# Seven block products for the half-wide last chunk of three gated networks

## The chip, the cores and the metric

The kernel runs on one NeuronCore of a Trainium2 chip. The metric is the device time of one execution in microseconds (us). Before the change it is 1073.06 us, the median of 3 runs (1071.64 to 1073.41). Names of engines: PE is the matrix engine (PEld its weight loads), DVE the vector engine, ACT the scalar engine, POOL the general one, SP the queue that issues most DMAs.

## The reference, cut to what matters

The model has two layers. Each layer has two gated networks ("nets"), one at its start and one at its end, with a mixer and a cross attention between them. So there are four nets in all. The change touches the last three. All is in float32, with 256 tokens, width 1024 and an inner width of 2816:

```python
D_MODEL, SEQ, DEPTH, D_FF = 1024, 256, 2, 2816

def swiglu(x, w_gate, w_up, w_down):
    return (jax.nn.silu(x @ w_gate) * (x @ w_up)) @ w_down

for l in range(DEPTH):
    h = layer_norm(ALPHA * h + 0.5 * swiglu(h, ffn1_gate[l], ffn1_up[l], ffn1_down[l]), ...)
    ...                                   # mixer, cross attention
    h = layer_norm(ALPHA * h + 0.5 * swiglu(h, ffn2_gate[l], ffn2_up[l], ffn2_down[l]), ...)
```

## The kernel before, in words

**Products in three parts.** A float32 number is split into a high part (rounded to the matrix engine's fp32r format) and a low part (the rest). `split` (lines 61 and 62) does that: ACT casts the high part (`whi`), then DVE subtracts it from the source (`wlo`). A product is then high x high + high x low + low x high. Every weight tile of 128x1024 that comes from memory (`raw`, 512 KB, 6 buffers) costs one cast on ACT and one subtraction on DVE before PE can use it; there are 8 buffers each of `whi` and `wlo`. A raw buffer is free for the next load once DVE has read it for the last time.

**A net in chunks.** The inner width of 2816 is cut into chunks of 512 columns: five whole ones (numbers 0 to 4) and a last one (number 5) of 256. For each chunk PE computes x @ gate and x @ up, the result is activated and multiplied, and `turn` (line 446) turns it so that it can be the left operand of the down product: four DMAs deal it to other partitions (line 450), DVE transposes it (line 453), and it is split again (`ah`, `al`). The down product of a chunk goes in slabs of 256 inner columns (two raw tiles, 24 matmuls), `both(c, u)`. The order at the end of a net is written in the loop over chunks: chunk 4, slabs (2,1) and (3,0), chunk 5, slab (3,1), and then the tail with the three slabs (4,0), (4,1) and (5,0). In the tail each of the four output blocks (two halves of the tokens by two halves of the columns) takes its 6 matmuls of the first slab, 6 of the second and 6 of the third before the next block begins. After the first two blocks the first half of the tokens is normalised, and after the other two the second half (`finish`, line 303 on).

**Ways to do a chunk.** A whole chunk goes either directly (`hidden`, 96 matmuls of 512 columns) or by seven block products (`by_seven`, line 555). The latter is Strassen's scheme in Winograd's form on 2x2 blocks: x and the pair of gate and up are cut into halves of tokens, of model width, and into gate and up. Instead of eight products of blocks there are seven, of weights that are sums of blocks, against blocks of x that were summed beforehand (`blocks_of_x`). Each product is 12 matmuls (`run`, line 597). `parts_of` makes the weights of one product: it adds a second block where the product needs a sum (line 584, DVE, in place in the raw tile) and splits the result. `put` (line 606) makes the half sums of the seven results on DVE; the first copy is ACT's (line 612). What comes after the last product (the last three sums, the activation, the multiplication and `turn`) is in `left`, which the loop calls after the slab (c - 2, 1). Nets 2 to 4 do chunks 2 and 4 by seven (`sevens`, line 666), net 1 chunk 4 alone.

**The last chunk before the change** is `last_hidden` (line 641): it takes the weights as the left operand (`mm_cols`), so its result is turned already and needs neither DMAs nor transposes. Each of its four `mm_cols` is 8 matmuls of 512 columns and 8 of 256. It splits four raw tiles.

**The order of the work.** Each engine works off its instructions in an order that a planner fixes when the kernel is built: by the program's order as the priority, with an instruction held back until the planner expects its inputs. Where `manual_schedule` stands in the code, the program's order holds.

## Time and profile before

| what | value |
|---|---|
| median of 3 runs | 1073.06 us |
| the profiled execution | 1072.23 us |
| its span, first to last instruction | 1070.2 us |
| granted clock of PE | 0.998 |
| DVE, ACT, POOL busy | 946.3, 642.2, 65.0 us |
| mean DMA rate | 217 GB/s |

The profile gives times from the span's start. A line such as "L62" is line 62 of the kernel. A row of the timeline has the start, the time from the start to the end of the merged group, engine, line, operation, output<-inputs, shapes and count, and in brackets how long the engine had been idle and what it waited for. Rows of stretches ("A:B") have the length, then the busy time of each engine with its number of instructions, the granted clock, the DMA engines' busy share and GB/s. Chunk 5 of the four nets starts on PE at 146.41, 505.08, 672.71 and 1031.37 us.

### The profile page before, as it was taken

The numbers are of one execution on the slowest core, as the hardware profiler recorded it, in microseconds if no ns is written. First come the engines' busy times: TensorE is split into PE (matmuls) and PEld (weight loads), VectorE is DVE, ScalarE is ACT, GpSimd is POOL, SyncE is SP. The second block draws the span as 40 slices with busy tenths as digits, with TensorE's granted clock in tenths as the row PEclk, the third lists the DMA queues.
The fourth block names the chain that finished last, engine by engine and source line by source line (L and its number), as shares of the span: only waits on it lengthen the run. The fifth ranks groups of instructions, "written<-read, shape, count | busy, mean of one in ns | idle before, by whom it ended". The sixth has DMA issues, their size and how long they took to land.

```text
span 1070.2 us, 16314 instructions
## 1 busy us (share of the span) xinstructions
PE 1060.6 (99%) x5968; PEld 938.9 (88%) x5968; DVE 946.3 (88%) x1318; ACT 642.2 (60%) x916; POOL 65.0 (6%) x114
## 2 busy tenths in 40 slices
PE   9999999999999999999999999999999999999997
PEld 7888888889899888888888888888898998888886
DVE  6977997998998799999799999788989787999986
ACT  7556655767457565656575557566764665656660
POOL 9600001000000000000000000010000000000000
PEclk9999999999999999999999999999999999999999
DMA  9998395755575575948675875957536665759471
GB/s 360 259 298 269 119 281 167 251 188 159 177 271 168 181 247 198 292 167 226 236 260 192 250 261 173 298 168 227 190 128 208 247 230 176 259 151 341 133 220 40
DMA packets 130896, 231.90 MB, mean 217 GB/s; under 512 B 9409, under 2 KB 48609, under 8 KB 130817
## 3 DMA queue, kind: packets, MB, share of 16 engines
q1 hardware_dynamic: 129024, 228.49, 65.6%
q0 software_dynamic: 1216, 1.20, 0.5%
q8 instruction: 47, 0.77, 0.3%
q10 hardware_dynamic: 576, 1.18, 0.3%
q14 instruction: 33, 0.26, 0.1%
HBM read 216.15 MB, written 1.05 MB: 203 GB/s over the span
## 4 chain that ended last, share of the span: by engine, by line
PE 99%; DMA 0%; DVE 0%; issue 0%; DVEq 0%
PE acc L105 65%; PE dn L105 31%; PE acc L172 1%; PE dn L910 1%; DMA h<-in_x_dram 0%; PE dn L969 0%; PE dn L968 0%; PE dn L958 0%; PE acc L1034 0%; PE dn L472 0%; PE dn L875 0%; DVE h L358 0%; DVE h L353 0%; DVE st L338 0%; DVE h L326 0%
## 5 line engine op out<-in xcount | busy, mean ns | idle before, releaser
L61 ACT CAST whi<-raw 128x1024 fp32r<-128x1024 f32 (+1 forms) x438 | 442.4, 1042 | 199.3 <-DVE raw L584 54.7
L62 DVE TENSOR_TENSOR wlo<-raw,whi 128x1024 fp32r<-128x1024 f32 (+1 forms) x438 | 515.6, 1210 | 33.9 <-ACT whi L61 30.4
L105 PE MATMUL acc<-whi,xT 128*128 128x512 f32 x1032 | 312.9, 380 | 0.0
L105 PEld LDWEIGHTS acc<-whi,xT 128*128 128x128 f32 x1032 | 195.0, 189 | 27.5
L105 PE MATMUL acc<-wlo,xT 128*128 128x512 f32 x516 | 195.6, 379 | 0.0
L105 PE MATMUL acc<-xT,whi 128*128 128x512 f32 x576 | 142.2, 382 | 0.2
L105 PE MATMUL dn<-whi,ah 128*128 128x512 f32 x346 | 131.5, 380 | 0.0
L105 PE MATMUL dn<-wlo,ah 128*128 128x512 f32 x346 | 131.1, 379 | 0.0
L105 PE MATMUL dn<-whi,al 128*128 128x512 f32 x346 | 131.1, 379 | 0.0
L105 PEld LDWEIGHTS acc<-xT,whi 128*128 128x128 f32 x576 | 103.9, 190 | 12.5 <-ACT whi L61 0.7
L105 PEld LDWEIGHTS acc<-wlo,xT 128*128 128x128 f32 x516 | 97.5, 189 | 13.9
L105 PE MATMUL dn<-whi,xT 128*128 128x512 f32 x288 | 87.9, 381 | 0.0
L105 PEld LDWEIGHTS acc<-xT,wlo 128*128 128x128 f32 x576 | 75.5, 191 | 3.9
L105 PE MATMUL acc<-xT,wlo 128*128 128x256 f32 x576 | 75.9, 275 | 0.0
L105 PEld LDWEIGHTS dn<-wlo,ah 128*128 128x128 f32 x346 | 65.4, 189 | 9.2
L105 PEld LDWEIGHTS dn<-whi,al 128*128 128x128 f32 x346 | 65.4, 189 | 9.2
L105 PEld LDWEIGHTS dn<-whi,ah 128*128 128x128 f32 x346 | 65.4, 189 | 9.1
L584 DVE TENSOR_TENSOR raw<-raw 128x1024 f32<-128x1024 f32 x56 | 66.2, 1218 | 0.4
L350 POOL TENSOR_TENSOR rs<-rs,nhalf 128x1 f32<-128x1 f32 x16 | 14.9, 929 | 834.2 <-DVE rs L346 598.7
L105 PEld LDWEIGHTS dn<-whi,xT 128*128 128x128 f32 x288 | 54.6, 190 | 7.4
L105 PE MATMUL dn<-wlo,xT 128*128 128x512 f32 x144 | 54.6, 379 | 0.0
L332 DVE SCALAR_TENSOR_TENSOR h<-h,dn 128x512 f32<-128x512 f32 x31 | 21.2, 683 | 31.6 <-PE dn L105 31.6
(232 smaller groups left out, 1278.7 us busy)
## 6 DMA issues: line engine op xcount, KB each, us to landing
raw<-in_ffn_up_dram SPq DMA_DIRECT2D x88, 512.0 KB, 5.3
raw<-in_ffn_down_dram SPq DMA_DIRECT2D x88, 512.0 KB, 6.9
raw<-in_ffn_gate_dram SPq DMA_DIRECT2D x84, 512.0 KB, 5.0
raw<-in_w_in_dram SPq DMA_DIRECT2D x48, 512.0 KB, 4.7
dealt<-sg SPq DMA_DIRECT2D x80, 128.0 KB, 4.7
raw<-in_ca_k_dram SPq DMA_DIRECT2D x16, 512.0 KB, 5.1
raw<-in_w_out_dram SPq DMA_DIRECT2D x16, 512.0 KB, 4.3
raw<-in_ca_v_dram SPq DMA_DIRECT2D x16, 512.0 KB, 5.3
```

Of the source, the lines that this page charges most:

```text
L61: nc.scalar.copy(hi, src)
L62: lows.append(nc.vector.tensor_tensor(lo, src, hi.bitcast(F32), op=ALU.subtract))
L105: nc.tensor.matmul(o, w, x, start=start, stop=stop)
L172: nc.tensor.transpose(pt[:, k, :], src[:, (4 * j + k) * P : (4 * j + k + 1) * P], unit)
L332: nc.vector.scalar_tensor_tensor(v, v, ALPHA / scale, sums(y[i][n]), op0=ALU.mult, op1=ALU.add, accum_out=None if junk is None else st[:, ...
L350: nc.gpsimd.tensor_tensor(rs, rs, nhalf[:, 0:1], op=ALU.pow)
L584: nc.vector.tensor_tensor(r[i], r[i], plus[i], op=ALU.add)
L910: nc.tensor.matmul(o[g, hh, :], kc[:, hh, g], x, start=True, stop=True)
```

## The change

In nets 2 to 4 chunk 5 goes by seven as well. `by_seven` learns a width of 256: a block of weights (4 x 128 rows by 256 columns) then fits into a single raw tile, so each of the four blocks takes one of the six raw buffers, and the tiles that the whole chunks borrow (`spare0` to `spare2`, `lng`, `lnb`) aren't needed for weights. The half sums `e` and `f` go to `spare0` and `spare1` there, which are tiles of raw weights in the whole chunks. `turn` learns half the width. `last_hidden` remains for net 1.

```diff
-            def turn(s):
+            def turn(s, n=4):
                 ah, al = act_tiles()
-                x = fp.tile([P, 4, NT, P], F32, tag="dealt", name="dealt", bufs=1)
+                x = fp.tile([P, 4, NT, 32 * n], F32, tag="dealt", name="dealt", bufs=1)
                 for a in range(4):
-                    nc.sync.dma_start(x[a * 32 : a * 32 + 32], s[:, :, a * P : (a + 1) * P])
+                    nc.sync.dma_start(x[a * 32 : a * 32 + 32], s[:, :, a * 32 * n : (a + 1) * 32 * n])
...
             def by_seven(c0, bx):
+                ncol = min(CHUNK, DFF - c0)
+                whole = ncol == CHUNK
+                def block(m, j, *tags):
+                    to = []
+                    per = 2 if whole else 4
+                    for i, g in enumerate(tags if whole else tags[0:1]):
+                        r = (fp if "spare" in g else wp).tile([P, DM], F32, tag=g, name="raw", bufs=6 if g == "raw" else 1)
+                        r = r.rearrange("p (k c) -> p k c", c=ncol)
+                        a = (4 * j + per * i) * P
                         loads.append(nc.sync.dma_start(
-                            to[i], m[k * P : (k + 2) * P, c0 : c0 + CHUNK].rearrange("(k p) c -> p k c", p=P)
+                            r, m[a : a + per * P, c0 : c0 + ncol].rearrange("(k p) c -> p k c", p=P)
                         ))
...
-                w00 = block(gate, 0, pieces("spare0", "spare1"))
-                w01 = block(up, 0, pieces("lng", "lnb"))
-                w11 = block(up, 1, pieces("raw", "raw"))
-                w10 = block(gate, 1, pieces("spare2", "raw"))
+                w00 = block(gate, 0, *(("spare0", "spare1") if whole else ("raw",)))
+                w01 = block(up, 0, *(("lng", "lnb") if whole else ("raw",)))
+                w11 = block(up, 1, "raw", "raw")
+                w10 = block(gate, 1, *(("spare2", "raw") if whole else ("raw",)))
...
+                sums_of = [
+                    fp.tile([P, 4, P], F32, tag="up", name="half").rearrange("p k t -> p (k t)") if whole
+                    else fp.tile([P, DM], F32, tag=f"spare{n}", name="half", bufs=1)[:, 0:ncol] for n in range(2)
+                ]
...
-            sevens = (2, 4) if early is None else (4,)
+            sevens = (2, 4, 5) if early is None else (4,)
...
-                if c == max(sevens) + 1:
+                if c == len(chunks) - 1:
                     gb = ln_params(l, n)
```

The rest of the diff writes `ncol` for the fixed width of 512 in `run`, `parts_of` and `left`.

More of the change, by code (lines that the diff above doesn't have):

```diff
@@ L440, in gated @@
                     nc.vector.tensor_tensor(v, o, v, op=ALU.mult)
-            def turn(s):
+            def turn(s, n=4):
                 ah, al = act_tiles()
-                x = fp.tile([P, 4, NT, P], F32, tag="dealt", name="dealt", bufs=1)
+                x = fp.tile([P, 4, NT, 32 * n], F32, tag="dealt", name="dealt", bufs=1)
                 for a in range(4):
-                    nc.sync.dma_start(x[a * 32 : a * 32 + 32], s[:, :, a * P : (a + 1) * P])
+                    nc.sync.dma_start(x[a * 32 : a * 32 + 32], s[:, :, a * 32 * n : (a + 1) * 32 * n])
                 for i in range(NT):
-                    d = fp.tile([P, 4, P], F32, tag="up", name="square")
+                    d = fp.tile([P, 4, P], F32, tag="up", name="square")[:, 0:n, :]
                     nc.vector.transpose(
-                        d.rearrange("p k (b r) -> p b k r", b=4), x[:, :, i, :].rearrange("p b (k j) -> p b k j", k=4)
+                        d.rearrange("p k (b r) -> p b k r", b=4), x[:, :, i, :].rearrange("p b (k j) -> p b k j", k=n)
                     )
-                    split(ah[:, :, tok(i)], al[:, :, tok(i)], d)
+                    split(ah[:, 0:n, tok(i)], al[:, 0:n, tok(i)], d)
                 return ah, al
@@ L555, in by_seven @@
             def by_seven(c0, bx):
-                def rows_by_columns(r):
-                    return r.rearrange("p (k c) -> p k c", c=CHUNK)
-                def pieces(*tags):
-                    return [
-                        rows_by_columns(
-                            (fp if "spare" in g else wp).tile([P, DM], F32, tag=g, name="raw", bufs=6 if g == "raw" else 1)
-                        )
-                        for g in tags
-                    ]
-                def block(m, j, to):
-                    for i in range(2):
-                        k = 4 * j + 2 * i
+                ncol = min(CHUNK, DFF - c0)
[7 more added lines that the diff above has]
+                        a = (4 * j + per * i) * P
                         loads.append(nc.sync.dma_start(
-                            to[i], m[k * P : (k + 2) * P, c0 : c0 + CHUNK].rearrange("(k p) c -> p k c", p=P)
+                            r, m[a : a + per * P, c0 : c0 + ncol].rearrange("(k p) c -> p k c", p=P)
                         ))
+                        to.append(r)
                     return to
-                w00 = block(gate, 0, pieces("spare0", "spare1"))
-                w01 = block(up, 0, pieces("lng", "lnb"))
-                w11 = block(up, 1, pieces("raw", "raw"))
-                w10 = block(gate, 1, pieces("spare2", "raw"))
+                w00 = block(gate, 0, *(("spare0", "spare1") if whole else ("raw",)))
+                w01 = block(up, 0, *(("lng", "lnb") if whole else ("raw",)))
+                w11 = block(up, 1, "raw", "raw")
+                w10 = block(gate, 1, *(("spare2", "raw") if whole else ("raw",)))
                 def parts_of(r, plus=None):
                     hi, lo = [], []
-                    for i in range(2):
+                    for i in range(len(r)):
                         if plus is not None:
@@ L586, in parts_of @@
                         w = wp.tile([P, 1024], F32R, tag="wlo", name="wlo", bufs=8)
-                        h, w = (rows_by_columns(x) for x in (h, w))
+                        h, w = (x.rearrange("p (k c) -> p k c", c=ncol) for x in (h, w))
                         split(h, w, r[i])
@@ L590, in parts_of @@
                         lo.append(w)
-                    return Weights(hi, lo, 2, [])
+                    return Weights(hi, lo, 4 // len(r), [])
                 def part_of_x(i, j):
@@ L598, in run @@
                     for k in range(4):
-                        wh, wl = w.at(k, slice(0, CHUNK))
+                        wh, wl = w.at(k, slice(0, ncol))
                         mm_rows(o, x[0][:, k, :], x[1][:, k, :], wh, wl, k == 0, k == 3)
+                sums_of = [
+                    fp.tile([P, 4, P], F32, tag="up", name="half").rearrange("p k t -> p (k t)") if whole
+                    else fp.tile([P, DM], F32, tag=f"spare{n}", name="half", bufs=1)[:, 0:ncol] for n in range(2)
+                ]
                 def half_sum():
-                    return fp.tile([P, 4, P], F32, tag="up", name="half").rearrange("p k t -> p (k t)")
+                    return sums_of.pop(0)
                 def put(o, a, op, b):
@@ L608, in by_seven @@
                 s = activations()
-                g = [s[:, i, :] for i in range(NT)]
-                o = [acc((P, CHUNK)) for _ in range(4)]
+                g = [s[:, i, 0:ncol] for i in range(NT)]
+                o = [acc((P, ncol)) for _ in range(4)]
                 run(o[0], part_of_x(0, 0), parts_of(w00))
@@ L621, in by_seven @@
                 put(e, o[2], ALU.subtract, e)
-                o = [acc((P, CHUNK)) for _ in range(3)]
+                o = [acc((P, ncol)) for _ in range(3)]
                 run(o[0], bx[3], parts_of(w11))
@@ L631, in left @@
                         put(g[i], o[1 + i], ALU.add, g[i])
-                    s = fp.tile([P, NT, CHUNK], F32, tag="spare2", name="sg", bufs=1)
+                    s = fp.tile([P, NT, CHUNK], F32, tag="spare2", name="sg", bufs=1)[:, :, 0:ncol]
                     for i, u in enumerate((e, f)):
@@ L636, in left @@
                         nc.vector.tensor_tensor(v, v, u.rearrange("p (k a j) -> p k a j", a=4, j=32), op=ALU.mult)
-                    return turn(s)
+                    return turn(s, ncol // P)
                 return left
```

## The prediction

> **What bounds the kernel now.** I read the page's first part and its chain first, then the table of stretches around chunk 5, then the timelines of PE, DVE, ACT and SP there.

> ```profile
> PE 1060.6 (99%) x5968; PEld 938.9 (88%) x5968; DVE 946.3 (88%) x1318; ACT 642.2 (60%) x916; POOL 65.0 (6%) x114
> PE 99%; DMA 0%; DVE 0%; issue 0%; DVEq 0%
> ```

> PE is busy for 99% of the span and is the whole chain: what takes a matmul away shortens the kernel, as long as nothing else becomes late. DVE at 88% is the one that can. The mean says little, so here is the end of a net by stages (net 4; chunk 4 by seven, slabs (2,1) and (3,0), chunk 5), and chunk 5 of nets 2 and 3:

> ```profile
> 1002.88:1021.01 18.13, 18.13 (x85) 15.88 (x84) 18.13 (x21) 14.85 (x17) 0.00 (x0) 1.00 0.55 175
> 1021.01:1031.37 10.36, 10.36 (x49) 9.07 (x48) 10.36 (x12) 5.25 (x6) 0.00 (x0) 1.00 0.87 232
> 1031.37:1041.85 10.48, 10.48 (x65) 9.62 (x64) 7.73 (x11) 6.89 (x11) 0.00 (x0) 1.00 0.84 272
> ...
> 505.08:515.56 10.48, 10.48 (x66) 9.62 (x64) 7.79 (x11) 6.86 (x11) 0.00 (x0) 1.00 1.04 334
> 672.71:683.19 10.48, 10.48 (x66) 9.62 (x64) 7.76 (x11) 6.62 (x11) 0.00 (x0) 1.00 1.00 325
> ```

> After the length come PE, PEld, DVE and ACT. DVE works without a pause through chunk 4 and the two slabs behind it (18.13 of 18.13, 10.36 of 10.36). Chunk 5 is the first stretch in which it has air (7.73 of 10.48). The three nets agree, so I work in net 4's times and multiply by three.

> **PE's gain.** Chunk 5 holds PE for 10.48 us: four times 8 matmuls of 512 and 8 of 256 columns. By seven it is 7 x 12 = 84 matmuls of 256. What such a matmul costs with a new left operand each time is shown by 24 in a row in the attention:

> ```profile
> 847.90 0.27 PE L105 MATMUL dn<-kTh,qTh 128*128 128x256 f32 x1
> ...
> 850.58 0.38 PE L105 MATMUL acc<-xT,whi 128*128 128x512 f32 x1
> ```

> (850.58 - 847.90) / 24 = 0.112 us. So 84 x 0.112 = 9.38 us, and PE saves **1.10 us per net**, 3.3 us in all. That is the most the change can bring.

> **DVE's price.** Steps are taken from start to start, since queued DVE instructions overlap a little:

> ```profile
> 1023.36 2.35 DVE L62 TENSOR_TENSOR wlo<-raw,whi 128x1024 fp32r<-128x1024 f32 x2
> 1025.63 0.68 DVE L636 TENSOR_TENSOR sg<-sg,half 128x512 f32<-128x512 f32 x1
> 1026.23 5.76 DVE L62 TENSOR_TENSOR wlo<-raw,whi 128x1024 fp32r<-128x1024 f32 x5
> 1033.57 1.23 DVE L62 TENSOR_TENSOR wlo<-raw,whi 128x1024 fp32r<-128x1024 f32 x1 [1.58 <-ACT whi L61]
> 1035.04 1.30 DVE L453 STREAM_TRANSPOSE square<-dealt 128x512 f32<-128x512 f32 x2 [0.24 <-DMA dealt<-sg]
> 1036.27 0.39 DVE L126 TENSOR_TENSOR sg<-acc,sg 128x256 f32<-128x256 f32 x1
> 1036.58 1.27 DVE L62 TENSOR_TENSOR al<-square,ah 128x512 fp32r<-128x512 f32 x2
> 1038.27 1.23 DVE L62 TENSOR_TENSOR wlo<-raw,whi 128x1024 fp32r<-128x1024 f32 x1 [0.42 <-ACT whi L61]
> 1039.41 0.42 DVE L126 TENSOR_TENSOR sg<-acc,sg 128x256 f32<-128x256 f32 x1
> 1039.75 1.22 DVE L62 TENSOR_TENSOR wlo<-raw,whi 128x1024 fp32r<-128x1024 f32 x1
> 1041.47 1.23 DVE L62 TENSOR_TENSOR wlo<-raw,whi 128x1024 fp32r<-128x1024 f32 x1 [0.51 <-ACT whi L61]
> ...
> 1044.53 0.69 DVE L652 TENSOR_TENSOR sg<-up,sg 128x512 f32<-128x512 f32 x1
> 1045.14 1.22 DVE L62 TENSOR_TENSOR wlo<-raw,whi 128x1024 fp32r<-128x1024 f32 x1
> 1046.28 1.64 DVE L62 TENSOR_TENSOR al<-sg,ah 128x256 fp32r<-128x256 f32 x2
> 1047.76 0.76 DVE L319 SCALAR_TENSOR_TENSOR h<-h,dn 128x512 f32<-128x512 f32 x1
> ...
> L584 DVE TENSOR_TENSOR raw<-raw 128x1024 f32<-128x1024 f32 x56 | 66.2, 1218 | 0.4
> ```

> The group of five gives (5.76 - 1.22) / 4 = 1.135 us for a subtraction of 128x1024, and the sums of blocks (L584, 1218 ns each like the subtractions) cost the same. An operation of 128x256 steps by 1039.75 - 1039.41 = 0.34 us.

> Removed per net: four L126 (1.4 us), the multiplication L652 (0.6) and the two splits behind it (1.5), together 3.5 us. Added: three more subtractions, since seven products need seven splits where four tiles needed four, and four sums of blocks, 7 x 1.135 = 7.9; seven half sums of 128x256, 2.4; two multiplications, two subtractions for `al` and two transposes of half the width, 6 x 0.34 = 2.0 (the transposes are not shown at this width; at full width one is 0.61, so at most 0.5 more). Together 12.4, so DVE has **8.9 us more per net**.

> [...]

> ACT gets three more casts, some 3.1 us, where it is busy for 6.89 of 10.48 us: I cost this at nothing. Its cover is that pause; without it the subtractions behind the casts would be as much later.

> **How much DVE has to spare.**

> ```profile
> 1024.50:1047.92 23.42, 23.42 (x126) 20.95 (x125) 20.64 (x26) 13.50 (x19) 0.00 (x0) 1.00 0.64 194
> 1049.62 0.38 PE L105 MATMUL dn<-whi,ah 128*128 128x512 f32 x1
> ```

> Counting the subtractions back from the net's last (1045.14, slab (5,0)), chunk 5's first is the second of the pair at 1023.36, so chunk 5 begins on DVE at 1024.50. From there to its last `al` at 1047.92 DVE works 20.64 us and idles 2.8. The tail's third slab, the first work that needs chunk 5's result, starts at 1049.62, so DVE is 1.7 us early. After the change the work is 20.64 + 8.9 = 29.5 us: not done before 1054.0 even without a pause, while PE would like to start that slab at 1048.5. Two waits follow.

> First, at the seventh product. DVE must have done, from 1024.50, seven splits and four sums (12.5), chunk 4's multiplication, transposes and splits (0.6 + 1.2 + 1.2) and four half sums (1.4): 16.9 us, so 1041.4. PE would start it at 1031.37 + 72 x 0.112 = 1039.4. **Wait 2.0 us**; the product ends at 1042.8, slab (3,1) at 1048.0, the tail's first two slabs (12 matmuls of 512 columns at 0.216 us, the step of 48 in 10.36 us above) at 1050.6. What is late then is chunk 5's result.

> Second, at the tail's third slab:

> ```profile
> 1022.27 3.85 SPq L77 DMA_DIRECT2D raw<-in_ffn_down_dram  x3
> 1026.34 2.71 SPq L450 DMA_DIRECT2D dealt<-sg  x4
> 1029.16 4.31 SPq L77 DMA_DIRECT2D raw<-in_ffn_down_dram  x5
> ...
> DMA to landing us min/median/max: 2.9/4.7/9.9
> ...
> 1032.49 1.05 ACT L61 CAST whi<-raw 128x1024 fp32r<-128x1024 f32 x1 [2.89 <-DMA raw<-in_ffn_down_dram]
> ```

> The last line but one is that of the tile `sg`. `last_hidden` had no such DMAs; `left` has. Behind the seventh product DVE owes (3,1)'s two splits (2.3), three half sums (1.0), (4,0)'s splits (2.3) and the multiplications (0.7), so the fourth deal (2.71 / 4 = 0.68 us of SP each) is issued at about 1041.4 + 6.3 + 3 x 0.68 = 1049.7. With the quickest landing, 2.9 us, it is there at 1052.6; transpose, cast and subtraction add some 1.3: 1053.9, as DVE's own sum says. The raw tiles say the same: the four blocks hold four of six buffers until their last use, two of them to the seventh product. Already now a down tile lands some 6.5 us after its issue (the third of the group at 1022.27, whose issue ends at 1026.1, and ACT's cast that waits for it until 1032.49). Tiles freed at 1041.4 and by (3,1) at 1042.6 and 1043.7 return as (4,1) and (5,0) at 1048 to 1050, and are split by 1051 to 1053.

> So the third slab starts at 1053.9 in place of 1049.62: **4.3 us later per net** if PE simply waits, with the 1.1 us already counted. Of the second wait, 3.3 us, a part can be filled: the next block's 12 matmuls of the first two slabs (2.6 us) need nothing of chunk 5. PE leaves the program's order nowhere in this trace, but it never had to; DVE is visibly planned by readiness. With all 2.6 us filled it is 1.7 us per net, with none 4.3. The rows name no nearer case, and I take the middle, **3.0 us per net, 9.0 us in all**. SP's four more issues (2.5 us) stand in front of the next stage's loads in nets 2 and 3; they have 13 us of tail as cover, and would cost their own 2.5 us without it.

> **The sum.** The profiled execution took 1072.23 us (span 1070.2 and 2.0 around it), 0.8 below the median of 1073.06. 1072.2 + 9.0 = **1081.2 us**.

> **Rivals.**
> - *DVE's lag is absorbed* (faster). DVE idles 2.8 us in that stretch and was ahead by 1.7 us; if the planner also orders the half sums so that the seventh split isn't held up (1.4 + 2.4 us of chunk 4's turn could go behind it), the first wait goes, and a well filled tail hides the second. Then only PE's 1.1 us counts: 1072.2 - 3.3 = 1068.9. It decides where DVE's work between 1024.5 and the third slab is under some 24 us. Against it stands the sum of 29.5 us. Chance 0.13.
> - *A wash*: the first wait remains by half and the second is filled, +0.5 us per net: 1073.7, with 1071 to 1075 around it. For it speaks that 10.4 us of the tail's matmuls don't need chunk 5; against it, that blocks finished later push the normalisation back. Chance 0.16.
> - *The deal is late, PE waits in order*: chunk 4's squares were issued from 1026.34 on and taken at 1035.04, 6 us after the last issue. With 6.0 in place of 2.9 us it is 4.3 + 3.1 = 7.4 us per net: 1094.4. In net 4 nothing else loads by then, which speaks against it. Chance 0.15.

> **Chances and range.** The forecast, with the second wait filled anywhere from fully to not at all (5.1 to 13 us in all, 1077 to 1085.5, and some way toward the late deal), has 0.56. A measurement of this kernel tells about 0.2% (2.1 us) from no change. Faster by more: 0.13; within: 0.16; slower: 0.71. The range leaves out the faster rival and half of the late one: 1071.5 to 1091, and the forecast's own is 1076 to 1088.

> **What would show it.** Per changed net 84 matmuls of 128x256 with a step of 0.112 us and 9.4 us of PE work; DVE busy without a pause from chunk 4 until the tail; PE idle before the seventh product (released by DVE `wlo` or ACT `whi`) and before the tail's third slab (released by `ah`, `al` or slab (5,0)); the deal of four 64 KB squares issued near 18 us after chunk 5's start and landing within 3 us. Wrong would be a DVE with pauses of over 2 us per net there, or PE without a gap: then the lag was absorbed. If PE's gaps are there but span more than 5 us per net, the deal or the raw buffers are the cause and not DVE's sum.

## The result, and the profile after

The changed kernel takes 1090.28 us (median of 6 runs, 1088.99 to 1095.61), the kernel before 1073.07 us beside it (6 runs). The ratio is 1.0174, 95% interval 1.0161 to 1.0186: it is **slower by 17.2 us**. I had forecast 1081.2 us: the sign was right, and so was the first of the two places, but the size was half of what came.

From the page of the changed kernel: busy time by engine, the chain that ended last, and the group of the sums of weight blocks.

```profile
PE 1065.4 (98%) x6028; PEld 940.9 (86%) x6028; DVE 972.0 (89%) x1357; ACT 644.7 (59%) x919; POOL 66.7 (6%) x114
...
PE 69%; DVE 20%; issue 5%; DMA 3%; ACT 2%; DVEq 0%; ACTq 0%; SPq 0%
...
L582 DVE TENSOR_TENSOR raw<-raw 128x1024 f32<-128x1024 f32 x68 | 81.0, 1219 | 0.8
```

DVE's share of the chain, 0% before, is 20%. It has 972.0 - 946.3 = 25.7 us more work, 8.6 us per net (I had 8.9); the sums (L584 before, L582 now) went from 56 to 68. ACT is no busier in sum (644.7 against 642.2 us).

The table of stretches of the changed kernel, with length, busy PE, PEld, DVE, ACT, POOL, the granted clock, DMA share and GB/s. In pairs for nets 2, 3 and 4: chunk 5 with its products, then the 24 matmuls or so behind it; then most of net 4's tail; then the place at which nets 2 and 3 transpose their normalised half.

```profile
505.20:519.69 14.49, 11.89 (x87) 10.88 (x86) 13.31 (x18) 9.87 (x12) 0.00 (x0) 0.95 0.43 132
519.69:525.40 5.71, 5.71 (x24) 4.86 (x24) 5.71 (x9) 3.83 (x6) 0.00 (x0) 0.84 0.92 284
680.33:694.22 13.89, 11.13 (x87) 10.12 (x86) 12.59 (x18) 9.12 (x12) 0.00 (x0) 1.00 0.40 118
694.22:699.00 4.78, 4.78 (x25) 4.19 (x24) 4.78 (x8) 3.95 (x6) 0.00 (x0) 1.00 0.87 323
1044.12:1058.66 14.54, 11.73 (x88) 10.72 (x86) 13.25 (x18) 9.72 (x12) 0.00 (x0) 0.96 0.38 119
1058.66:1064.40 5.74, 5.74 (x23) 4.86 (x23) 5.74 (x9) 4.11 (x6) 0.00 (x0) 0.81 0.75 267
1064.40:1076.14 11.74, 11.74 (x57) 10.27 (x55) 7.61 (x14) 1.77 (x3) 0.00 (x0) 1.00 0.06 14
540.60:544.40 3.80, 1.73 (x12) 0.93 (x10) 3.70 (x9) 3.66 (x7) 0.92 (x1) 1.00 0.87 272
714.20:717.90 3.70, 1.63 (x12) 1.02 (x11) 3.66 (x8) 3.56 (x7) 2.04 (x6) 1.00 0.70 238
```

Three losses can be read off.

**The products wait.** In net 3 the stretch holds 84 matmuls of 256 columns and two of 512 that the planner drew in, 84 x 0.112 + 2 x 0.216 = 9.84 us of work in 13.89: 4.05 us are lost. DVE is busy for 12.59 of it. PE's timeline in net 4:

```profile
1050.14 0.38 PE L105 MATMUL acc<-wlo,kTh 128*128 128x256 f32 x1 [0.39 <-DVE wlo L62]
...
1052.81 0.38 PE L105 MATMUL acc<-wlo,xT 128*128 128x256 f32 x1 [0.75 <-DVE wlo L62]
...
1055.36 0.38 PE L105 MATMUL acc<-whi,xT 128*128 128x256 f32 x1 [1.05 <-ACT whi L61]
1056.31 0.70 PE L105 MATMUL dn<-whi,ah 128*128 128x512 f32 x2 [0.57 <-ACT whi L61]
1056.84 0.27 PE L105 MATMUL acc<-wlo,xT 128*128 128x256 f32 x1
1056.95 0.39 PE L105 MATMUL acc<-whi,xT 128*128 128x256 f32 x2
...
1058.23 0.42 PE L105 MATMUL acc<-wlo,xT 128*128 128x256 f32 x1
1058.45 0.42 PE L105 MATMUL acc<-whi,xT 128*128 128x256 f32 x1
```

PE waits at the fifth product, at the sixth (1052.81), and around the seventh three times (before 1055.36, before 1056.31, and for its low part at 1056.84, which it bridges with two matmuls of slab (3,1)). DVE's timeline beside it says why:

```profile
1042.99 1.22 DVE L582 TENSOR_TENSOR raw<-raw 128x1024 f32<-128x1024 f32 x1
1045.41 2.36 DVE L62 TENSOR_TENSOR wlo<-raw,whi 128x1024 fp32r<-128x1024 f32 x2 [1.19 <-ACT whi L61]
1047.68 1.30 DVE L453 STREAM_TRANSPOSE square<-dealt 128x512 f32<-128x512 f32 x2
1048.91 1.18 DVE L62 TENSOR_TENSOR wlo<-raw,whi 128x1024 fp32r<-128x1024 f32 x1
1050.01 1.28 DVE L62 TENSOR_TENSOR al<-square,ah 128x512 fp32r<-128x512 f32 x2
...
1051.54 1.22 DVE L62 TENSOR_TENSOR wlo<-raw,whi 128x1024 fp32r<-128x1024 f32 x1
...
1053.01 1.22 DVE L582 TENSOR_TENSOR raw<-raw 128x1024 f32<-128x1024 f32 x1
...
1055.34 3.50 DVE L62 TENSOR_TENSOR wlo<-raw,whi 128x1024 fp32r<-128x1024 f32 x3
```

Ahead of 1045.41 DVE stands idle for 1.19 us, with all its later work still to do: the sum for the third product ends at 1044.21, only then can ACT cast it, and only then can DVE subtract. From there to the last row no row has a bracket: DVE goes from one piece of due work to the next. The subtraction of the sixth product starts at 1051.54, behind chunk 4's transposes and splits; the sum for the seventh starts at 1053.01, ACT's cast can follow only then, and the subtraction after that only at 1055.34.

**The clock falls** behind the waits in nets 2 and 4 (0.84 and 0.81, against 1.00 in net 3): at 1058.23 a matmul of 256 columns steps by 0.22 us, at 1056.84 by 0.11.

**The normalised half is late** in nets 2 and 3: of 3.80 and 3.70 us PE works 1.73 and 1.63. Here are the transposes behind net 2 on PE's timeline, first in the kernel before (no bracket, so no wait), then in the changed one. There the matmul ahead of them starts at 540.67:

```profile
533.69 1.04 PE L172 MATMUL acc<-pdn,h 128*128 128x128 f32 x8
```

```profile
543.02 1.38 PE L172 MATMUL acc<-pdn,h 128*128 128x128 f32 x8 [1.97 <-DVE h L358]
```

Per net, in us. The clock's part is (1 - clock) times the length of both stretches of the pair, and is taken off the products' waits; "measured" is how much later the next chunk 5 (for net 4 the end of the span) comes than before, counted from this one.

| | net 2 | net 3 | net 4 |
|---|---|---|---|
| PE's saving | -1.1 | -1.1 | -1.1 |
| waits of the products | 3.9 | 4.05 | 4.1 |
| lowered clock | 1.6 | 0 | 1.7 |
| normalised half late | 2.1 | 2.1 | none |
| sum | 6.5 | 5.05 | 4.7 |
| measured | 7.5 | 5.1 | 5.45 |

The measured row adds up to 18.1 us, as the spans differ (1088.4 - 1070.2 = 18.2). Some 1.9 us, in nets 2 and 4, are not in the table. Of net 4's, 0.75 lie behind the last matmul: from its start to the end of the span it is 1070.2 - 1062.59 = 7.6 us before and 1088.4 - 1080.04 = 8.4 after. In net 2, 0.55 lie in the transposes themselves, which take 1.34 us from their start to the next product (543.02 to 544.36) instead of 0.79 (533.69 to 534.48). The last 0.6 us I can't assign to a place.

### The profile page after: what moved, and what is told of

It reads as the page before. It is cut to its first block, busy times and chain, and to the rows that moved or that the text cites. A ratio compares the mean times of both kernels' runs of the same rounds, so it can differ in the third digit from the quotient of the medians.

```text
span 1088.4 us, 16509 instructions
## 1 busy us (share of the span) xinstructions
PE 1065.4 (98%) x6028; PEld 940.9 (86%) x6028; DVE 972.0 (89%) x1357; ACT 644.7 (59%) x919; POOL 66.7 (6%) x114
## 3 DMA queue, kind: packets, MB, share of 16 engines
HBM read 216.15 MB, written 1.05 MB: 200 GB/s over the span
## 4 chain that ended last, share of the span: by engine, by line
PE 69%; DVE 20%; issue 5%; DMA 3%; ACT 2%; DVEq 0%; ACTq 0%; SPq 0%
PE acc L105 46%; PE dn L105 20%; DVE wlo L62 9%; DVE raw L582 5%; ACT whi L61 2%; DMA raw<-in_ffn_down_dram 2%; PE acc L172 1%; DVE half L609 1%; DVE square L453 1%; DMA raw<-in_ffn_up_dram 1%; DVE sg L609 1%; DVE al L62 1%; PE dn L913 1%; DVE sg L440 1%; DMA h<-in_x_dram 0%
## 5 line engine op out<-in xcount | busy, mean ns | idle before, releaser
L61 ACT CAST whi<-raw 128x1024 fp32r<-128x1024 f32 (+1 forms) x447 | 449.1, 1041 | 220.1 <-DVE raw L582 91.7
L62 DVE TENSOR_TENSOR wlo<-raw,whi 128x1024 fp32r<-128x1024 f32 (+1 forms) x447 | 525.7, 1209 | 32.3 <-ACT whi L61 28.4
L105 PE MATMUL acc<-whi,xT 128*128 128x512 f32 (+1 forms) x1104 | 329.2, 375 | 3.6 <-ACT whi L61 3.5
L105 PEld LDWEIGHTS acc<-whi,xT 128*128 128x128 f32 x1104 | 207.6, 190 | 33.5 <-ACT whi L61 4.4
L105 PE MATMUL acc<-wlo,xT 128*128 128x512 f32 (+1 forms) x552 | 206.6, 374 | 2.3 <-DVE wlo L62 2.3
L105 PE MATMUL dn<-whi,ah 128*128 128x512 f32 x346 | 131.2, 381 | 1.7 <-ACT whi L61 1.7
L105 PE MATMUL dn<-wlo,ah 128*128 128x512 f32 x346 | 132.2, 382 | 0.0
L105 PE MATMUL dn<-whi,al 128*128 128x512 f32 x346 | 132.2, 382 | 0.0
L105 PEld LDWEIGHTS acc<-wlo,xT 128*128 128x128 f32 x552 | 105.0, 190 | 17.0 <-DVE wlo L62 3.2
L105 PE MATMUL acc<-xT,whi 128*128 128x512 f32 x480 | 119.0, 383 | 0.1
L105 PEld LDWEIGHTS acc<-xT,whi 128*128 128x128 f32 x480 | 86.5, 190 | 10.1 <-ACT whi L61 0.4
L105 PE MATMUL dn<-whi,xT 128*128 128x512 f32 x288 | 87.8, 381 | 0.0
L582 DVE TENSOR_TENSOR raw<-raw 128x1024 f32<-128x1024 f32 x68 | 81.0, 1219 | 0.8
L105 PEld LDWEIGHTS dn<-whi,ah 128*128 128x128 f32 x346 | 65.5, 190 | 11.5 <-ACT whi L61 2.3
L105 PEld LDWEIGHTS dn<-wlo,ah 128*128 128x128 f32 x346 | 66.2, 191 | 9.4
L105 PEld LDWEIGHTS dn<-whi,al 128*128 128x128 f32 x346 | 66.0, 191 | 9.4
L105 PEld LDWEIGHTS acc<-xT,wlo 128*128 128x128 f32 x480 | 62.9, 191 | 3.2
L105 PE MATMUL acc<-xT,wlo 128*128 128x256 f32 x480 | 63.3, 275 | 0.0
L105 PEld LDWEIGHTS dn<-whi,xT 128*128 128x128 f32 x288 | 54.3, 189 | 7.4
L105 PE MATMUL acc<-wlo,kTh 128*128 128x512 f32 (+1 forms) x160 | 56.0, 350 | 0.9 <-DVE wlo L62 0.9
L105 PE MATMUL acc<-whi,kTh 128*128 128x512 f32 (+1 forms) x160 | 55.7, 348 | 0.0
```

What stands on the lines that cost most here:

```text
L61: nc.scalar.copy(hi, src)
L62: lows.append(nc.vector.tensor_tensor(lo, src, hi.bitcast(F32), op=ALU.subtract))
L105: nc.tensor.matmul(o, w, x, start=start, stop=stop)
L582: nc.vector.tensor_tensor(r[i], r[i], plus[i], op=ALU.add)
```

## The experiments

The experiments were to decide between two theories. **A, the chain**: each of the last products goes DVE, ACT, DVE (sum, cast, subtraction), and the hand-overs between the engines make PE wait. **B, the queue**: DVE has more work than air in that stretch, and where the lateness shows is incidental. All differences are of medians, against the kernel before in the same set of runs.

**The sum in two pieces** (theory A's remedy: ACT can cast the first half while DVE sums the second; the casts and subtractions of chunk 5 go in two pieces too).

```diff
+                        cuts = (slice(0, r[i].shape[1]),) if whole else (slice(0, 2), slice(2, 4))
+                        for c in cuts:
+                            if plus is not None:
+                                nc.vector.tensor_tensor(r[i][:, c, :], r[i][:, c, :], plus[i][:, c, :], op=ALU.add)
+                            split(h[:, c, :], w[:, c, :], r[i][:, c, :])
```

> Chunk 5's sums, casts and subtractions go in two pieces of 128x512 instead of one of 128x1024. Theory A (the new wait inside chunk 5 is a chain through one raw tile: sum, cast, subtraction, 1.22 + 1.05 + 1.22 us in turn, where a whole chunk has two tiles that overlap): the chain's step falls to about 2.4 us, PE's gaps inside chunk 5 fall from 4.0 to under 2 us per net, and the time to 1083 to 1086 us. Theory B (DVE simply has too much work): DVE pays some 0.07 us more for each of 11 extra instructions, the gaps stay at 4 to 5 us, 1090 to 1093 us.

1087.65 us, +15.3 (ratio 1.0137, 1.0122 to 1.0152): 2 us better than the change. The waits around the last products shrink, but others come up at slab (3,1), and the normalised half waits as long:

```profile
522.81 0.48 PE L105 MATMUL dn<-wlo,ah 128*128 128x512 f32 x1 [0.42 <-DVE wlo L62]
...
540.70 1.47 PE L172 MATMUL acc<-pdn,h 128*128 128x128 f32 x8 [1.97 <-DVE h L358]
```

The time lies between the two ranges. A shorter chain won 2 us, and most of the lateness came up in other places.

**Without the sums of chunk 5** (the kernel leaves out the four sums of weight blocks in chunk 5, so its products use single blocks).

```diff
-                        if plus is not None:
+                        if plus is not None and whole:
```

> Leaves out the four sums of weight blocks in chunk 5 of nets 2 to 4 (so part of the weights is missing there), nothing else. DVE has 4.5 us less per net and no chain of sums. Theories A and B: the gaps of 4.0 us inside chunk 5 go, and with them the clock drop behind them in nets 2 and 4 (1.6 us each): 1073 to 1077 us. If the wait before the transposes of the first half of the tokens (2.1 us in nets 2 and 3) stays, it is the deal's landing (theory C); if it falls below 1 us, it was DVE's lateness.

1071.52 us, -0.9 (0.9995, 0.9985 to 1.0004). The losses of the changed kernel go: no wait in chunk 5 of nets 2 and 4 and no lowered clock (the row is net 4's, with chunk 5 from 1031.06 on), and the transposes behind net 2 wait 0.2 us.

```profile
1030.00:1044.00 14.00, 14.00 (x107) 13.44 (x106) 14.00 (x22) 11.07 (x14) 0.00 (x0) 1.00 0.65 230
```

Taking away 4.5 us of DVE's work per net takes away 18 us in three nets, but this removes a link of the chain and load alike, so it doesn't decide between A and B. And even with the sums free the scheme only equals the kernel before. In the profiled execution net 4 keeps its 1.1 us; what the other two win is taken back by waits of 0.2 to 0.5 us, at the transposes and in net 3's chunks 2 and 5.

**Without the deal** (chunk 5's four DMAs are left out, the transposes take the undealt tile).

```diff
-                for a in range(4):
-                    nc.sync.dma_start(x[a * 32 : a * 32 + 32], s[:, :, a * 32 * n : (a + 1) * 32 * n])
+                if n == 4:
+                    for a in range(4):
+                        nc.sync.dma_start(x[a * 32 : a * 32 + 32], s[:, :, a * 32 * n : (a + 1) * 32 * n])
```

> Leaves out the four deal DMAs of chunk 5 in nets 2 to 4: the transposes read the undealt rows, so the layout is wrong there. Theory C (the tail's third slab is late because of the deal): chunk 5's result is there 4 to 6 us earlier, the wait before the transposes of the first half of the tokens falls from 2.1 to under 0.5 us, total 1084 to 1086 us; the gaps inside chunk 5 stay at 4.0 us. Against it (DVE's queue or the down tiles make the third slab late): the wait stays above 1.5 us and the time within 1088 to 1091 us.

1086.09 us, +13.7 (1.0133, 1.0116 to 1.015). The wait of the normalised half is gone, as theory C had it, and the time is at the edge of its range. But one of 1.4 us stands in the tail instead, for a subtraction:

```profile
527.26 0.48 PE L105 MATMUL dn<-wlo,ah 128*128 128x512 f32 x1 [1.38 <-DVE wlo L62]
```

So my late-deal rival can carry some 3.5 us of the price at most.

**The change in net 4 alone.**

```diff
-            sevens = (2, 4, 5) if early is None else (4,)
+            sevens = ((2, 4, 5) if last else (2, 4)) if early is None else (4,)
```

> The change in net 4 alone; nets 2 and 3 as before. If the three nets' prices add up, net 4 costs 5.4 us (its share of the 18.2 us in the profile): 1078 to 1079 us. If part of net 4's price is inherited from net 2 and 3, it is under 4 us.

1075.15 us, +2.8 (1.0033, 1.002 to 1.0046). The waits of the products are all there (3.9 us with the small ones), the clock stays at 1.00, nothing is normalised for a next net: 3.9 - 1.1 = 2.8. I had expected 5.4, a third of the whole. Missing is what the column of net 4 above has beside the products' waits: the lowered clock (1.7) and the 0.75 that it leaves out. The profiled execution took 1077.11 us, 2 us above the median; 1.2 of that is a wait in net 1 (at 131.68), which the edit does not touch.

**Chunk 4's turn later** (its transposes and splits stand behind chunk 5's splits in the program).

```diff
+                if apart:
+                    put_off.append(rest_of)
+                else:
+                    rest_of()
...
+                    while c == 5 and put_off:
+                        put_off.pop()()
```

> The transposes and splits of chunk 4's result (2.4 us of DVE) stand behind chunk 5's sums and splits in the program; all else as changed. Theory B (DVE's queue sets the waits in chunk 5): PE's gaps in chunk 5 fall from 4.0 to about 1.6 us per net, total 1080 to 1085 us. Theory A (the chain through the one tile sets them): the gaps stay above 3 us, 1088 to 1091 us.

1087.08 us, +15.2 (1.014, 1.0125 to 1.0155), 2 us better than the change and between the two ranges. The waits in chunk 5 fall to some 1.6 us in net 2, as theory B had it, but one of 0.8 appears at slab (3,1), and the normalised half waits longer:

```profile
517.60 0.48 PE L105 MATMUL dn<-wlo,ah 128*128 128x512 f32 x1 [0.64 <-DVE wlo L62]
540.13 1.97 PE L172 MATMUL acc<-pdn,h 128*128 128x128 f32 x8 [2.40 <-DVE h L358]
```

The first rival's idea (the seventh split ahead of chunk 4's turn) was tried with this: it wins 2 us and moves the rest.

**Two of the sums on POOL** (for the fourth and the seventh product).

```diff
-                run(o[3], bx[2], parts_of(w01, w11))
+                run(o[3], bx[2], parts_of(w01, w11, *aside_adds))
...
-                run(o[2], part_of_x(1, 1), parts_of(w00, w10))
+                run(o[2], part_of_x(1, 1), parts_of(w00, w10, *aside_adds))
```

> The sums of weight blocks for chunk 5's fourth and seventh products go to POOL (idle there), the other two stay on DVE. DVE has 2.3 us less per net. Theory B: gaps in chunk 5 fall from 4.0 to about 2 us, 1083 to 1086 us, if POOL adds 128x1024 in under 3 us. Theory A: the seventh product's chain gets longer by what POOL is slower, so no gain: 1089 to 1092 us. If POOL and DVE hinder each other, the DVE operations beside it become longer than 1.22 us and the time rises.

1089.14 us, +17.2 (1.0159, 1.0144 to 1.0174): nothing won, as theory A had it. POOL's timeline, and DVE's beside it:

```profile
500.99 2.38 POOL L582 TENSOR_TENSOR raw<-raw 128x1024 f32<-128x1024 f32 x1 [125.84 <-DVE raw L582]
508.20 3.30 POOL L582 TENSOR_TENSOR raw<-raw 128x1024 f32<-128x1024 f32 x1 [4.83 <-DVE wlo L62]
```

```profile
502.06 2.40 DVE L62 TENSOR_TENSOR wlo<-raw,whi 128x1024 fp32r<-128x1024 f32 x1 [1.20 <-ACT whi L61]
...
510.40 2.18 DVE L62 TENSOR_TENSOR wlo<-raw,whi 128x1024 fp32r<-128x1024 f32 x1
```

A sum takes 2.4 to 3.3 us on POOL instead of 1.2, and the DVE subtraction that overlaps it takes 2.40 and 2.18 us instead of 1.22. What DVE was spared, two sums or 2.4 us per net, it loses again nearly whole (2.1 us), so this doesn't decide either.

**Chunk 5 by seven behind a direct chunk 4**, and as its partner **chunk 2 alone by seven**. A direct chunk 4 gives DVE a lead, while chunk 5 keeps the same chain.

```diff
-            sevens = (2, 4, 5) if early is None else (4,)
+            sevens = (2, 5) if early is None else (4,)
```

> Chunks 2 and 5 by seven in nets 2 to 4, chunk 4 directly: DVE comes to chunk 5 with a lead, as it has some 20 us less to do for chunk 4. To be read against the next kernel (chunk 2 alone by seven, chunk 5 as before the change). Theory B: with that lead chunk 5 by seven has no gaps, and it is 3 us faster than the next kernel. Theory A: gaps of 2 us and more remain in chunk 5 in spite of the lead, and it is not faster than the next kernel.

```diff
-            sevens = (2, 4, 5) if early is None else (4,)
+            sevens = (2,) if early is None else (4,)
```

> Chunk 2 alone by seven in nets 2 to 4, chunk 5 as before the change. Chunk 4 directly costs PE 96 x 0.216 = 20.7 in place of 18.1 us: 2.6 us more per net, so 1080 to 1081 us in all theories, unless DVE's load cost PE something before.

1080.23 us (+8.3; 1.0077, 1.006 to 1.0094) and 1079.57 us (+7.7; 1.0071, 1.0055 to 1.0086). With the lead, chunk 5 by seven takes exactly my 9.38 us, without any wait (first row: its chunk 5 in net 2). But net 3's chunk 2, by seven as before, loses 2.5 us around its last two products:

```profile
507.05:516.43 9.38, 9.38 (x85) 9.37 (x84) 9.34 (x12) 8.37 (x11) 0.00 (x0) 1.00 0.75 231
```

```profile
602.45 0.48 PE L105 MATMUL acc<-wlo,xT 128*128 128x512 f32 x1 [0.45 <-DVE wlo L62]
604.73 0.48 PE L105 MATMUL acc<-whi,xT 128*128 128x512 f32 x1 [0.94 <-ACT whi L61]
605.68 0.70 PE L105 MATMUL dn<-whi,ah 128*128 128x512 f32 x2 [0.46 <-ACT whi L61]
```

Between the two kernels chunk 5's change should have won 3.3 us; it lost 0.7, so B's 3 us did not come, nor did A's gaps in chunk 5. With a lead the chain alone makes no wait there: DVE's lateness is needed for it. The partner kernel has no wait in net 3's chunk 2. It is tempting to take this one, 85 us later, for the lateness of net 2's chunk 5 handed on. But DVE stands idle in between, for 4.20 us at the end of net 2 and for 2.2 more around 570, so its queue had caught up:

```profile
530.02 0.69 DVE L332 SCALAR_TENSOR_TENSOR h<-h,dn 128x512 f32<-128x512 f32 x1 [4.20 <-PE dn L105]
```

The order of DVE's work in that chunk 2 differs between the two kernels; that this makes the wait is not shown.

**DVE's load alone, twice.** The kernel before, PE's work untouched, with extra DVE operations in chunk 5 of nets 2 to 4 that nobody reads: eight (9.1 us), or two per loop pass in place of four, so four (4.6 us).

```diff
+                    load_ = fp.tile([P, DM], F32, tag="spare0", name="more", bufs=1)
+                    nc.gpsimd.memset(load_, 0.0)
...
+                    for _ in range(4 if early is None else 0):
+                        nc.vector.tensor_tensor(load_, load_, load_, op=ALU.max)
```

> The kernel before, with chunk 5 as four direct tiles and PE's work untouched; eight more DVE operations of 128x1024 (the larger of a tile and itself, read by nobody, some 9 us, the 8.9 us that I worked out for the change) stand in chunk 5 of nets 2 to 4. Theory B (DVE's lag alone makes the price): PE waits in and behind chunk 5 as in the changed kernel, 4 to 6 us per net in nets 2 and 3 and somewhat less in net 4: 1083 to 1091. Theory A (it is the chain of the seven products and the squares): DVE catches up in its pauses and in the tail, where PE has 10 us of work that need nothing of DVE: 1073 to 1077.

> The kernel before with four more DVE operations of 128x1024 in chunk 5 of nets 2 to 4 (4.6 us) in place of eight (9.1 us, 3.45 us of price per net). If DVE's air there (1.7 us of lead and 2.8 us of pauses, 4.5 in all) is free and only what lies above it is paid, as I worked out: 1071.5 to 1074. If DVE's work there is paid in proportion: 1076 to 1078.

Eight: 1082.03 us, +10.4 (1.0098, 1.0083 to 1.0113). Four: 1071.57 us, -0.3 (0.9998, 0.9989 to 1.0007). PE's timeline with eight, at its longest wait behind chunk 5 of net 2:

```profile
523.95 0.48 PE L105 MATMUL dn<-wlo,ah 128*128 128x512 f32 x1 [1.45 <-DVE wlo L62]
```

So 4.6 us are free, and of 9.1 us some 3.5 are paid per net, a microsecond under B's range in all. The load alone makes about half of what the change costs: 10.4 of 17.2 + 3.3 = 20.5 us (PE's gain of 3.3 counted back). But it makes it in another place. In the profiled execution no wait stands in chunk 5 or slab (3,1); PE waits 2.3 to 3.2 us per net in the tail, for subtractions, and in net 2 the clock falls behind them (0.88 from 520 to 526, 0.95 from 526 to 545). The waits of the products are thus not the load's alone. With the run before, in which the same chain with a lead makes none, they take both: a late DVE and the chain. How the second half of the price divides between the two, no run shows.

If every microsecond above the allowance is paid in full, the allowance is 9.1 - 3.5 = 5.6 us; I had read 2.8 + 1.7 = 4.5 from the trace. The tail's 10 us of PE work do not hide the load, since a late subtraction holds up the slabs that are next in PE's order.

**PE kept busy in the waits** (twenty matmuls of 128x256 that nobody reads).

```diff
+                def idle(n):
+                    for _ in range(0 if whole else n):
+                        nc.tensor.matmul(blank, xTh[:, 0, 0:P], xTh[:, 0, :], start=True, stop=True)
...
+                idle(8)
                 run(o[1], part_of_x(0, 1), parts_of(w10))
+                idle(12)
```

> Twenty matmuls of 128x256 that nobody reads stand in chunk 5 of nets 2 to 4, eight ahead of the sixth product and twelve ahead of the seventh, so that TensorE works through most of the idle time of the sixth and seventh product (1.02, 1.22 and 0.84 us). If the granted clock of 0.81 to 0.84 behind chunk 5 of nets 2 and 4 comes from the idle time, it stays at 1.00 there and 1.6 us per net come back in two nets: 1086 to 1088. If it comes from something else, the drop stays: 1090 to 1092. Theory A and B (the chain of sum, cast and subtraction; DVE's queue) expect the same beside it: the products wait as long as before.

1085.22 us, +13.6 (1.0126, 1.0111 to 1.0141), 3.6 us better than the change. The granted clock is 1.00 behind chunk 5 of net 2 (row) and throughout net 4's, and over the whole of each of the four executions it is 0.997 or 0.998 (the changed kernel: 0.990 to 0.995). With PE at work in the waits the drop does not come.

```profile
518.96:525.40 6.44, 6.44 (x32) 5.66 (x31) 6.44 (x9) 5.57 (x8) 0.00 (x0) 1.00 0.88 302
```

The wait of the normalised half had fallen too, to 0.3 us, which I had not expected: DVE's order there had come out otherwise. So this run doesn't tell how much of the 3.6 us is the clock's. That led to norm_first below.

**The half sums back in `up`.**

```diff
-                    else fp.tile([P, DM], F32, tag=f"spare{n}", name="half", bufs=1)[:, 0:ncol] for n in range(2)
+                    else fp.tile([P, 4, P], F32, tag="up", name="half").rearrange("p k t -> p (k t)")[:, 0:ncol] for n in range(2)
```

> One part of the change undone: the half sums of chunk 5 go back to the rotating tiles 'up' instead of spare0 and spare1. If the place of the half sums matters, they wait for chunk 4's squares, which use the same two buffers: 1092 to 1096. If DVE's queue is the bound, it is late anyway and they cost nothing: 1088.5 to 1091.5.

1090.94 us, +19.3 (1.0171, 1.0154 to 1.0188). The interval covers the change's ratio: their place shows no effect.

**Two raw buffers given back.**

```diff
-                w00 = block(gate, 0, *(("spare0", "spare1") if whole else ("raw",)))
-                w01 = block(up, 0, *(("lng", "lnb") if whole else ("raw",)))
+                w00 = block(gate, 0, *(("spare0", "spare1") if whole else ("lng",)))
+                w01 = block(up, 0, *(("lng", "lnb") if whole else ("lnb",)))
```

> Two of chunk 5's four raw blocks (w00, w01) lie in the tiles 'lng' and 'lnb', which are free there, so two of the six raw buffers stay with the slabs. The raw buffers, my prediction's third argument: the slabs' loads come earlier, ACT's three waits for them (0.37, 0.80, 1.99 us in net 4) go, and 1 to 3 us per net come back: 1083 to 1087. DVE's queue: the tiles are there earlier and DVE is as late: 1088.5 to 1091.

1088.45 us, +16.8 (1.0155, 1.014 to 1.017; the change 1.0161 to 1.0186, overlapping). ACT still waits for the down tiles in net 4, where PE has no wait any more:

```profile
1064.37 1.05 ACT L61 CAST whi<-raw 128x1024 fp32r<-128x1024 f32 x1 [1.53 <-DMA raw<-in_ffn_down_dram]
```

My third argument, the raw tiles, does not carry the price.

**The mean first.** In the changed kernel DVE's timeline at the end of net 2 is this:

```profile
535.48 0.69 DVE L332 SCALAR_TENSOR_TENSOR h<-h,dn 128x512 f32<-128x512 f32 x1 [4.14 <-PE dn L105]
...
536.09 1.22 DVE L62 TENSOR_TENSOR wlo<-raw,whi 128x1024 fp32r<-128x1024 f32 x1
537.23 0.68 DVE L332 SCALAR_TENSOR_TENSOR h<-h,dn 128x512 f32<-128x512 f32 x1
...
537.83 1.22 DVE L62 TENSOR_TENSOR wlo<-raw,whi 128x1024 fp32r<-128x1024 f32 x1
538.97 0.21 DVE L342 TENSOR_SCALAR mv<-st 128x1 f32<-128x1 f32 x1
```

Two subtractions for the next stage stand between the residual's halves and the mean (L342), 2.3 us, about the wait. DVE's queue is not behind here: the first bracket has it idle for 4.14 us, until PE ends the first block. The edit keeps the next stage's first four behind the mean, alone and together with the idle matmuls (norm_busy):

```diff
+        with tc.issue_after(behind.ins) if behind is not None else nullcontext():
             lows.append(nc.vector.tensor_tensor(lo, src, hi.bitcast(F32), op=ALU.subtract))
...
-                    split(h, w, r)
+                    split(h, w, r, mean.pop() if mean else None)
```

> The changed kernel, in which the first four weight subtractions of the stage behind nets 2 and 3 stand behind the net's mean in DVE's order (in the changed kernel two stand ahead of it and one right behind). If those subtractions are what makes PE wait 2.14 us for the normalised half in nets 2 and 3, the wait falls to some 0.4 us and 3 to 4 us go in all: 1086 to 1087.5. If the late squares or the late deal make it, it stays: 1089.5 to 1091.5.

> The edit of norm_first together with the twenty idle matmuls of kept_busy. If the lowered clock and the normalisation's wait are two separate prices (1.6 us in nets 2 and 4, 1.7 to 2.6 in nets 2 and 3), what is left is the products' waits alone, three times 4.0 - 1.1 = 8.7 us: 1080.5 to 1083. If kept_busy had already taken both, since its wait there was 0.44 us, it comes out as kept_busy: 1084.5 to 1087.

1090.28 us, +18.4 (1.0172, 1.0148 to 1.0196), and 1089.28 us, +17.4 (1.0166, 1.015 to 1.0181): neither expectation held. The time of norm_first is the one that I had put down for an unchanged wait, but the wait did change, and the gain was gone at once. PE's timeline of norm_first behind net 2:

```profile
539.21 1.38 PE L174 MATMUL acc<-pdn,h 128*128 128x128 f32 x8 [0.51 <-DVE h L363]
545.38 1.29 PE L174 MATMUL acc<-pdn,h 128*128 128x128 f32 x8 [1.29 <-DVE h L363]
547.08 0.48 PE L107 MATMUL acc<-wlo,xT 128*128 128x512 f32 x1 [0.42 <-DVE wlo L64]
```

The first half's wait fell from 1.97 to 0.51 us; the second half now waits 1.29 and the next stage's weights 0.42. The deferred subtractions are still owed, and the waits come back just behind. The lowered clock and the late half are therefore not two prices that could be struck off one by one.

## Why the prediction was wrong, by its steps

- **PE's gain**, 1.10 us per net by 84 steps of 0.112: right. With DVE ahead, the stretch is 9.38 us long.
- **DVE's price**, 8.9 us per net: right (8.6 measured as busy time). The step of 1.135 us held as well: the extra operations of dve_load come at 1.13 us.
- **DVE's air**, 2.8 us of pauses and 1.7 of lead: somewhat small. Four operations more (4.6 us) cost nothing.
- **The first wait, 2.0 us at the seventh product: the step that failed first.** It is 4.0 us, at the last three products. I added up DVE's work to the seventh split, 16.9 us without a pause, and so had it done 1041.4 - 1031.37 = 10.0 us after PE's start of chunk 5. In net 4 it is done 1055.34 + 1.22 - 1044.12 = 12.4 us after it. Of the 2.4 us, 1.2 are the pause ahead of 1045.41, in which DVE waits for ACT's cast behind the third product's sum. I had put the casts at nothing, as ACT was far from busy; but in this chain a cast stands between two pieces of DVE's work. Another 0.8 us are DVE's later start: it begins chunk 5 at 1038.06, 6.1 us ahead of PE and not 6.9. PE's waits at the fifth and the sixth product are part of the same 4.0 us; without them it would have waited so much longer at the seventh.
- **The second wait, 3.3 us, half filled:** the filling was complete. The tail in net 4 holds PE for 11.74 of 11.74 us, and the deal's four issues run from 1061.33 - 1044.12 = 17.2 to 20.5 us after chunk 5's start (I had put them near 18). SP's row:

```profile
1061.33 3.29 SPq L450 DMA_DIRECT2D dealt<-sg  x4
```

  But what had been put into the gap was the next block's work, and so the first half's sums came later, with the next stage's subtractions planned in between: 2.1 us at the transposes of nets 2 and 3. I had named this in the wash rival ("blocks finished later push the normalisation back") and given it no price.
- **The clock** was in no term: 1.6 us in nets 2 and 4. PE's waits cost more than their length there.
- **The signs:** gaps of over 5 us per net were to accuse the deal or the raw buffers. They are 6 us in nets 2 and 3 (3.9 + 2.1 and 4.05 + 2.1), but with two raw buffers given back the time stays, and without the deal 13.7 us of 17.2 stay. This sign would have misled. And DVE was to work without a pause from chunk 4 to the tail; the pause of 1.19 us is the one priced above.
- **The rivals:** absorption was refuted by dve_load, and its order of work won only 2 us in late_turn; the wash left out the first wait's true size. The late deal gave 1094.4, nearer in number than the forecast, but by another mechanism. That the time lies within the widest range (1071.5 to 1091), which was opened toward this rival, is luck; the forecast's own, 1076 to 1088, it missed.

Per net, without PE's gain, the forecast's price was 3.0 + 1.1 = 4.1 us; measured is (17.2 + 3.3) / 3 = 6.8. Of that the products' waits are 4.0, the lowered clock 1.1 on average, the late half 1.4, and the remaining 0.3 is of what the table leaves out. That DVE's added work causes the price is shown (no_sums, and both loads); how much of it is plain load and how much the chain stays open.

No version beat the kernel before; the one with the sums left out only equals it.

## What to carry over

Before adding work to an engine that is off the critical path, find its allowance: an experiment with idle operations on that engine (here 4.6 us were free, and 3.5 were paid of 9.1) shows the load's part of the price without building the change. Where the added work passes from one engine to another and back, lay it out piece by piece: a sum of the one engine's work leaves out the pauses in which it waits for the other (here 1.2 us of DVE). And do not price the waits singly: three remedies that each shortened a wait won 0 to 2 us, as others came up behind it (in slab (3,1), the tail, the normalisation), so a remedy counts only by the whole time.

## What the hardware showed beside this

**The clock was halved behind a cluster of short waits.** None of the waits ahead of the drops in nets 2 and 4 was longer than 1.05 us by its bracket (1055.36 above), yet the step of a 128x256 matmul went from 0.11 to 0.22 us. Within the six executions of the changed kernel the slowest two have the lowest granted clock (1095.61 us at 0.990, 1092.49 at 0.994; the others 0.995). With PE kept busy it stayed at 1.00 behind chunk 5 (kept_busy). Stretches of 3.41 us show it closer; the first row is ahead of the drop in net 2, the second is the drop, the last is the place in net 3:

```profile
514.70:518.11 3.41, 1.79 (x12) 1.35 (x11) 3.31 (x6) 2.98 (x4) 0.00 (x0) 1.00 0.55 154
518.11:521.52 3.41, 3.41 (x14) 3.05 (x14) 3.41 (x6) 3.41 (x6) 0.00 (x0) 0.50 0.85 247
...
688.78:692.19 3.41, 1.87 (x12) 1.49 (x12) 3.30 (x7) 1.77 (x2) 0.00 (x0) 1.00 0.33 78
```

**POOL and DVE beside each other.** In pool_adds a float32 sum of 128x1024 took 2.38 and 3.30 us on POOL, and the DVE subtraction that ran beside it 2.40 and 2.18 instead of 1.22. Both times the subtraction ends 1.1 us after POOL's sum (504.45 and 503.37, 512.58 and 511.50), as if it had waited until then. POOL's longer sum is the one that started beside a running subtraction (until 509.26). The two transposes beside that sum (509.18) took 1.30 us together, as those of the kernel before did (1035.04).
